# A max-pooled 3x3 convolution on one core: ten instead of eleven five-product steps, joint row sums and differences, weight taps kept as neighbours, and a new order

## The chip, the cores and the metric

The kernel runs on one core of one Trainium2 chip. The metric is the device time of one execution in microseconds. TensorE (PE), VectorE (DVE), ScalarE (ACT), GpSimd (POOL) and SyncE (SP) each work through their own list of instructions in order and wait for one another by semaphores. Transfers between the chip's memory and the core are started from the lists of SP, POOL and ACT.

## The reference

`x` has 16 images of 64 channels and 64 x 64 points, `weight` 128 x 64 taps of 3 x 3, `pool_size` is 2. What is computed:

```python
x_pad = np.pad(x, ((0, 0), (0, 0), (1, 1), (1, 1)))
for kh in range(3):
    for kw in range(3):
        conv[b, co] += weight[co, ci, kh, kw] * x_pad[b, ci, kh:kh+h, kw:kw+w]   # over b, co, ci
output[b, c, i, j] = np.max(conv[b, c, 2*i:2*i+2, 2*j:2*j+2])
```

The output is 16 x 128 x 32 x 32 in float32.

## The kernel before

**Steps.** Two images lie in the 128 partitions at once (64 channels each, the two "halves" h = 0 and 1). The 16 images make 8 pairs, each pair is cut into 4 quarters of 16 input rows, and one quarter of one pair is a step: 32 steps, each giving 8 pooled rows of both images. For a pooled row, two rows of the convolution are needed. With the three rows of taps g0, g1, g2 and the input rows x(-1), x(0), x(1), x(2), they are a = g0 x(-1) + g1 x(0) + g2 x(1) and b = g0 x(0) + g1 x(1) + g2 x(2).

`TYPES` says how each step does it.

- A **K step** (five products): `PA1` = (g2 - g1) x(1) and `PA2` = g0 x(-1) go to one accumulator; `PB1` = (g0 - g1) x(0) and `PB2` = g2 x(2) to another. Then max(a, b) is the larger of the two plus `PR` = g1 (x(0) + x(1)). The products read the bf16 copy `kx` of the input, and only the sum `ks` is computed beforehand.
- A **W step** (four products, row-transformed): `P2` works on the difference `we` = x(0) - x(1), `P0` and `P3` on the differences `wd` of rows two apart, `P1` on the sum `ws` = x(0) + x(1). These three are made from the float32 copy `wx`.

A product is three taps in the width for each half: for one half three matmuls of 64 rows of weights by up to 512 points. `product` pairs a product of half 0 with a product of half 1 (not always the same one) and issues the six matmuls alternately, so that the two halves of TensorE work side by side. Below, a **pair of products** means these six matmuls.

**Accumulators.** There are eight (`acc`, 128 x 8 x 64 float32), handed out from the list `free`. `ta` holds the first sum of a step and half, `tb` the second. `evac` (EV, ScalarE) copies the first one to SBUF as `ev` and frees it; in a W step `seed` (SE, ScalarE) has copied the first product into `tb` before. `rowmax` (MX, VectorE) takes the maximum of `tb` and `ev` into `tb`; after it the last product (`PR` or `P1`) is added to `tb`. `odd` (OD, ScalarE) copies the odd columns, and `colmax` (CM, VectorE) takes the maximum of the even columns and that copy into `o`, frees the accumulator and, with the second half, starts the store from SP's list. A product that opens an accumulator therefore waits for the EV or CM that freed it, and `PR` and `P1` wait for their MX.

**Row sums and differences.** `ks` (KS) is on VectorE, one per K step; `ws` (WS) on VectorE, as a `tensor_tensor` or, for steps in `SUM_BY_REDUCTION`, as a `tensor_reduce`; `we` (E) on VectorE for steps in `DIFF_ON_VECTOR`, else on GpSimd; `wd` (D) on GpSimd. `on_gpsimd` puts a GpSimd operation behind the last VectorE `tensor_tensor` (or cast) written before it in the order, so that the two do not start together.

**Loads.** The weights, the first 33 rows of pair 0 (`kfirst`, `ksecond`) and the rows of the first W step come first, on SP's list. The further rows of W steps (L, LB) follow there; LB is held until a cast of `kfirst` is done. K steps after the first two get their rows by converting transfers from POOL's list (LK).

**Weights.** `g0`..`GP` write seven blocks of three taps (with zero slots or ring copies `u...` between) into `wq`; T... turns two neighbouring slots at a time on TensorE, so that half 0 uses the upper and half 1 the lower half of a turned column; V... copies the result to `wt`.

**Order.** Nothing is planned at run time. The string `ORDER` is a list written out by hand, such as `P2.4.0` (product P2 of step 4, half 0) or `CM.22.0`, and each engine's list is what its entries have in that order. Eight matmuls on constants run on TensorE while the weights arrive.

Of the kernel before, what the change touches and what calls it, by code (L numbers as in the profile page):

```python
# [11 lines left out]
def kernel(  # L12
# [37 lines left out]
    d_pool = ctx.enter_context(tc.tile_pool(name="d_pool", bufs=5))  # L50
    e_pool = ctx.enter_context(tc.tile_pool(name="e_pool", bufs=5))
    ws_pool = ctx.enter_context(tc.tile_pool(name="ws_pool", bufs=5))
    ks_pool = ctx.enter_context(tc.tile_pool(name="ks_pool", bufs=4))
# [13 lines left out]
    sbuf_op = [None]  # L67

# [28 lines left out]
    def wload(s, part=None):  # L97
# [4 lines left out]
        if part == 0:  # L102
            hi = 2 * R * q + R + 1
        elif part == 1:
            lo = 2 * R * q + R + 1
        return nc.sync.dma_start(out=wx[p % NWX][:, lo + 1 : hi + 1, :], in_=rows_of(p, lo, hi))
# [8 lines left out]
    klo2, khi2 = chunk(1)  # L115
    ksecond = const.tile([128, khi2 - klo2, W], FP32)
# [16 lines left out]
    BLOCKS = {"D2": 1, "G0": 5, "D0": 9, "G2": 13, "GM": 17, "G1": 21, "GP": 25}  # L133
    D2, G0, D0, G2, GM, G1, GP = BLOCKS.values()
    RING = ("GM", "G1", "GP")
    wq = const.tile([CO, 29, CI], BF16)
    wt = const.tile([128, 28, CO], BF16)
    gsum = const.tile([CO, 3, CI], FP32)
    for s in range(0, GM, 4):
        nc.gpsimd.memset(wq[:, s, :], 0.0)  # L140
# [8 lines left out]
    def ring(m):  # L149
        s = BLOCKS[m]  # L150
        nc.gpsimd.tensor_copy(out=wq[:, s + 3, :], in_=wq[:, s, :])  # L151

    def turned_cols(m):
        lo = BLOCKS[m] - (m not in RING)
# [15 lines left out]
    def turn_out(m):  # L170
# [3 lines left out]
        if m == "GM":  # L174
            nc.scalar.mul(dst, src, 0.5)
        elif m == "GP":
            nc.vector.tensor_scalar_mul(out=dst, in0=src, scalar1=0.5)
        elif m in ("G0", "G2"):
# [4 lines left out]
    def tap_of(m0, kw, half):  # L183
        if m0 in (GM, G1, GP):
            return m0 + (kw - half) % 3
        return m0 + kw - half

    def taps(t, h, m0, rows, start=False, skip=None, span=(0, R)):
# [7 lines left out]
        def one(kw):  # L196
            o0, o1, c0, c1 = (0, W, 0, W) if kw == 1 else (1, W, 0, W - 1) if kw == 0 else (0, W - 1, 1, W)
            if start and kw == 1:
# [3 lines left out]
                wt[lo : lo + CI, tap_of(m0, kw, h), :],  # L202
# [25 lines left out]
    def q_of(s):  # L228
        return place[s][1]
# [38 lines left out]
    def first_product(k, part):  # L268
        s, q = KSTEPS[0], 0
        m0, first, where, skip = (  # L270
            (D2, 1, ta, None),
            (G0, -1, ta, 0),
# [8 lines left out]
        pair_of_taps(where, s, m0, step2(kx_of(s), first), start, skip, span)  # L281


    def second_product(k, part):
        s = WSTEPS[0]
        if k == 0 and part == 0:
            take(ta, s, 0)
            take(ta, s, 1)
        m0, of, where = ((GM, "we", ta), (G0, "wd", ta), (G2, "wd", tb))[k]
        rows = step1(row[of, s]) if k == 0 else step2(row[of, s], k - 1)  # L290
        span = (0, R // 2) if part == 0 else (R // 2, R)
        pair_of_taps(where, s, m0, rows, k == 0 and part == 0, None, span)
# [4 lines left out]
    def ks(s):  # L297
        row["ks", s] = ks_pool.tile([128, R, W], BF16, name="ks")
        t, f = kx_of(s), 2 * R * q_of(s)
        on_vector(  # L300
            nc.vector.tensor_tensor(  # L301
                out=row["ks", s], in0=t[:, f : f + 2 * R : 2, :], in1=t[:, f + 1 : f + 2 * R : 2, :], op=ADD
            )
        )
# [5 lines left out]
    def ws(s):  # L310
        row["ws", s] = ws_pool.tile([128, R, W], BF16, name="ws")
        t, f = wx_rows(s)
        if s in SUM_BY_REDUCTION:
            with nc.allow_low_precision("bf16 operand of TensorE, as the other row sums"):
                nc.vector.tensor_reduce(  # L315
                    out=row["ws", s],
                    in_=t[:, f : f + 2 * R, :].rearrange("p (r two) w -> p r w two", two=2),
# [5 lines left out]
            nc.vector.tensor_tensor(  # L323
                out=row["ws", s], in0=t[:, f : f + 2 * R : 2, :], in1=t[:, f + 1 : f + 2 * R : 2, :], op=ADD
            )
        )

    def we(s):
        row["we", s] = e_pool.tile([128, R, W], BF16, name="we")
        t, f = wx_rows(s)  # L330
        vector = s in DIFF_ON_VECTOR
        inst = (nc.vector if vector else nc.gpsimd).tensor_tensor(  # L332
            out=row["we", s], in0=t[:, f : f + 2 * R : 2, :], in1=t[:, f + 1 : f + 2 * R : 2, :], op=SUB
# [3 lines left out]
    def wd(s):  # L337
        row["wd", s] = d_pool.tile([128, 2 * R, W], BF16, name="wd")
        t, f = wx_rows(s)
        on_gpsimd(  # L340
            nc.gpsimd.tensor_tensor(  # L341
                out=row["wd", s], in0=t[:, f + 1 : f + 1 + 2 * R, :], in1=t[:, f - 1 : f - 1 + 2 * R, :], op=SUB
            )
        )

    def we_half(part):
        s = WSTEPS[0]
        if part == 0:
            row["we", s] = e_pool.tile([128, R, W], BF16, name="we")
        t, f = wx_rows(s)  # L350
        lo, hi = f + R * part, f + R * (part + 1)
        on_vector(
            nc.vector.tensor_tensor(
                out=row["we", s][:, R // 2 * part : R // 2 * (part + 1), :],
                in0=t[:, lo:hi:2, :],
                in1=t[:, lo + 1 : hi : 2, :],
                op=SUB,
            )
        )

    def wd_half(part):
        s = WSTEPS[0]
        if part == 0:
            row["wd", s] = d_pool.tile([128, 2 * R, W], BF16, name="wd")
        t, f = wx_rows(s)
        lo, hi = f + R * part, f + R * (part + 1)
        on_gpsimd(
            nc.gpsimd.tensor_tensor(
                out=row["wd", s][:, R * part : R * (part + 1), :],
                in0=t[:, lo + 1 : hi + 1, :],  # L370
                in1=t[:, lo - 1 : hi - 1, :],
                op=SUB,
            )
        )

    def lk(n, part):
# [3 lines left out]
        if n == 0:  # L380
            inst = kload(0, *chunk(2 + part))
            if part == 0:
                behind(inst, sbuf_op[0])
# [6 lines left out]
    def late_load(s):  # L390
        behind(wload(s), sbuf_op[0])
# [21 lines left out]
    def seed_half(part, h):  # L413
        s = WSTEPS[0]
        span = slice(R // 2 * part, R // 2 * (part + 1))
        if part == 0:
            t = take(tb, s, h, fresh=False)
            if t in unset:
                unset.discard(t)
                nc.tensor.matmul(  # L420
                    acc[t], zeros[:, 0:128], zeros, start=True, stop=True, skip_group_check=True
                )
        nc.scalar.copy(out=acc[tb[s, h]][:, span, :], in_=acc[ta[s, h]][:, span, :])

# [8 lines left out]
    def colmax(s, h):  # L433
        if s not in ot:
            ot[s] = o_pool.tile([128, 2, R, WO], FP32, name="o")
        t = tb.pop((s, h))
        nc.vector.tensor_tensor(out=ot[s][:, h], in0=acc[t][:, :, 0::2], in1=od[s, h], op=MAX)  # L437
        free.append(t)
        made[s] = made.get(s, 0) + 1
        p, q = place[s]  # L440
        dst = out[2 * p : 2 * p + 2, :, q * R : (q + 1) * R, :].rearrange("b c h w -> c b (h w)")
        src = ot[s].rearrange("p b h w -> p b (h w)")
        if s == N - 1:
            store = nc.scalar if made[s] == 1 else nc.sync
# [3 lines left out]


    def cast_rows(lo, hi):  # L450
        on_vector(nc.vector.tensor_copy(out=kx[0][:, lo:hi:2, :], in_=kfirst[:, lo:hi:2, :]))  # L451

    def cast_more(first):
        dst, src = kx[0][:, klo2 + first : khi2 : 2, :], ksecond[:, first::2, :]
        if first in CAST_ON_VECTOR:
# [13 lines left out]
        "XOa": lambda: cast_rows(1, kmid),  # L469
        "XOb": lambda: cast_rows(kmid, khi),  # L470
        "XEa": lambda: cast_rows(0, kmid),
        "XEb": lambda: cast_rows(kmid + 1, khi),
        "X1": lambda: cast_more(0),
        "X2": lambda: cast_more(1),
        "F": first_product,
        "G": second_product,
        "Ea": lambda: we_half(0),
        "Eb": lambda: we_half(1),
        "Da": lambda: wd_half(0),
        "Db": lambda: wd_half(1),  # L480
        "SEa": lambda h: seed_half(0, h),
# [112 lines left out]
```

## Time and profile before

| | |
|---|---|
| three runs | 104.67, 104.80, 105.44 us (median 104.8) |
| the profiled execution | 105.15 us, of which the span of the instructions is 103.4 us |
| busy in the span | PE 97.2, DVE 92.0, ACT 82.2, POOL 75.6 us |
| mean granted TensorE clock | 0.993 |
| moved by transfers | HBM read 17.14 MB, written 8.39 MB |

The page of the profile lists, for groups of instructions, the mean time of one (from its start to its end) and the busy time of all; where instructions of one engine overlap, the distance from one start to the next is shorter than the mean. That distance is what fills an engine's list, and it is read from the timeline: four MX begin at 16.03 us and the next instruction at 18.47 us, so one MX takes 0.61 us of the list though it lasts 0.69 us. In the profile, MX is line 427, CM line 437, the matmuls of products line 200, OD line 431, EV lines 399 and 401, SE line 411, WS lines 315 (reduction) and 323, E line 332, D line 341, KS line 301.

### The profile page before, as it was taken

The page shows a single profiled execution, that of the slowest core. Times are in us where ns is not written, and L with a number is a line of the kernel's source. Part 1 is how long each engine was busy: PE and PEld are TensorE (multiplying, and loading weights), DVE is VectorE, ACT ScalarE, POOL GpSimd, SP SyncE. Part 2 cuts the span into 40 slices and gives each one's busy share as a digit, 9 for nine tenths or more (in the row PEclk, how much of TensorE's full clock was granted, in tenths as well). Part 3 has the DMA queues.
Part 4 walks back from the last instruction along what each step waited for, and adds up shares of the span by engine and source line. Part 5 has one row for each costly group of instructions (what it writes and reads, how often), then busy time and mean ns, then how long its engine had stood idle before and what let it go on. Part 6 is the DMA issues. An engine that isn't in the chain of part 4 may idle for free.

```text
span 103.4 us, 2541 instructions
## 1 busy us (share of the span) xinstructions
PE 97.2 (94%) x909; PEld 62.9 (61%) x909; DVE 92.0 (89%) x179; ACT 82.2 (79%) x181; POOL 75.6 (73%) x65
## 2 busy tenths in 40 slices
PE   6999799999999999999999999999999999999910
PEld 2497655555865465576666685556746777777600
DVE  1389899999999999999999999999989996979960
ACT  4546988886789997993887898987899898698820
POOL 6046869773995899998999997959997919970000
PEclk9999999999999999999999999999999999999997
DMA  2988999999999999999859992187699232006152
GB/s 62 299 312 262 360 291 268 349 416 404 248 194 298 286 318 339 351 340 204 163 159 261 312 384 101 56 205 263 176 154 257 81 136 101 0 13 233 65 202 102
DMA packets 13341, 23.33 MB, mean 226 GB/s; under 512 B 1040, under 2 KB 9488, under 8 KB 13328
## 3 DMA queue, kind: packets, MB, share of 16 engines
q1 hardware_dynamic: 12320, 20.68, 60.8%
q0 software_dynamic: 864, 2.36, 13.7%
q8 instruction: 7, 0.11, 0.4%
q10 hardware_dynamic: 144, 0.13, 0.4%
q14 instruction: 6, 0.05, 0.1%
HBM read 17.14 MB, written 8.39 MB: 247 GB/s over the span
## 4 chain that ended last, share of the span: by engine, by line
PE 91%; DVE 3%; issue 1%; DVEq 0%
PE acc L200 85%; PE acc L551 3%; PE acc L164 2%; DVE acc L427 2%; DVE o L437 1%; DVEq L589 0%; DVEq L437 0%; DVEq L427 0%
## 5 line engine op out<-in xcount | busy, mean ns | idle before, releaser
L200 PEld LDWEIGHTS <-wt 64*128 64x128 bf16 x876 | 59.6, 94 | 31.5 <-issue 1.5
L341 POOL TENSOR_TENSOR wd<-wx 128x1024 bf16<-128x1024 f32 x20 | 47.1, 2361 | 7.7 <-PE acc L200 3.4
L200 PE MATMUL acc<-wd,wt 64*128 64x504 bf16 (+3 forms) x264 | 50.1, 367 | 0.0
L200 PE MATMUL acc<-kx,wt 64*128 64x504 bf16 (+6 forms) x288 | 50.0, 356 | 0.0
L427 DVE TENSOR_TENSOR acc<-acc,ev 128x512 f32<-128x512 f32 x64 | 42.0, 691 | 1.1 <-ACT ev L401 0.3
L200 PE MATMUL acc<-we,wt 64*128 64x512 bf16 (+2 forms) x132 | 31.7, 367 | 0.0
L200 PE MATMUL acc<-ws,wt 64*128 64x504 bf16 (+1 forms) x126 | 28.7, 377 | 0.1
L401 ACT ACTIVATE ev<-acc 128x512 f32<-128x512 f32 x42 | 25.1, 608 | 2.7 <-PE acc L200 2.3
L431 ACT COPY od<-acc 128x256 f32<-128x256 f32 x64 | 22.5, 379 | 5.8 <-PE acc L200 5.2
L437 DVE TENSOR_TENSOR o<-acc,od 128x256 f32<-128x256 f32 x64 | 24.5, 416 | 2.1 <-ACT od L431 1.9
L411 ACT COPY acc<-acc 128x512 f32<-128x512 f32 x40 | 23.0, 581 | 3.0 <-PE acc L200 1.7
L332 POOL TENSOR_TENSOR we<-wx 128x512 bf16<-128x512 f32 x16 | 20.2, 1273 | 3.3 <-DVE ws L323 2.4
L200 PE MATMUL acc<-ks,wt 64*128 64x504 bf16 (+1 forms) x66 | 16.5, 377 | 0.5 <-DVE acc L427 0.5
L315 DVE TENSOR_REDUCE ws<-wx 128x512 bf16<-128x1024 f32 x11 | 13.5, 1229 | 0.0
L399 ACT COPY ev<-acc 128x512 f32<-128x512 f32 x22 | 12.9, 595 | 0.6 <-PE acc L200 0.6
L323 DVE TENSOR_TENSOR ws<-wx 128x512 bf16<-128x512 f32 x10 | 7.1, 723 | 0.0
L301 DVE TENSOR_TENSOR ks<-kx 128x512 bf16<-128x512 bf16 x11 | 4.6, 429 | 0.3 <-ACT kx L458 0.3
L551 PE MATMUL acc<-const-bfloat16-1.0 128*128 128x512 bf16 x8 | 3.6, 628 | 0.8 <-PEq L575 0.8
L95 POOL DMA_DIRECT2D kx<-in_x_dram x6 | 3.5, 587 | 0.7 <-DVE kx L451 0.7
L164 PEld LDWEIGHTS <-wq 128*128 128x128 bf16 x25 | 2.3, 132 | 1.4 <-issue 1.4
L151 POOL COPY wq<-wq 128x64 bf16<-128x64 bf16 x3 | 0.7, 241 | 3.1 <-ACT wq L462 2.5
L164 PE MATMUL acc<-ident,wq 128*128 128x128 bf16 x25 | 2.8, 285 | 0.0
(30 smaller groups left out, 22.3 us busy)
## 6 DMA issues: line engine op xcount, KB each, us to landing
out_dram<-o SPq DMA_DIRECT2D x31, 256.0 KB, 4.2
wx<-in_x_dram SPq DMA_DIRECT2D x10, 512.0 KB, 7.2
wx<-in_x_dram SPq DMA_DIRECT2D x5, 544.0 KB, 7.6
wx<-in_x_dram SPq DMA_DIRECT2D x5, 480.0 KB, 7.4
kx<-in_x_dram POOLq DMA_DIRECT2D x2, 528.0 KB, 7.4
ksecond<-in_x_dram SPq DMA_DIRECT2D x1, 512.0 KB, 7.0
kx<-in_x_dram POOLq DMA_DIRECT2D x2, 256.0 KB, 7.0
kx<-in_x_dram POOLq DMA_DIRECT2D x1, 496.0 KB, 12.0
```

What stands on the lines that cost most here:

```text
L164: nc.tensor.transpose(tp[:, (j - lo) * CO : (j - lo + 1) * CO], wq[:, j : j + 2, :].rearrange("a b c -> a (b c)"), ident,)
L200: nc.tensor.matmul(acc[t][:, i0:i1, o0:o1], wt[lo : lo + CI, tap_of(m0, kw, h), :], rows(lo, i0, i1, c0, c1), start=start and kw == 1, sto ...
L315: nc.vector.tensor_reduce(out=row["ws", s], in_=t[:, f : f + 2 * R, :].rearrange("p (r two) w -> p r w two", two=2), axis=mybir.AxisListTy ...
L323: nc.vector.tensor_tensor(out=row["ws", s], in0=t[:, f : f + 2 * R : 2, :], in1=t[:, f + 1 : f + 2 * R : 2, :], op=ADD)
L332: inst = (nc.vector if vector else nc.gpsimd).tensor_tensor(out=row["we", s], in0=t[:, f : f + 2 * R : 2, :], in1=t[:, f + 1 : f + 2 * R : ...
L341: nc.gpsimd.tensor_tensor(out=row["wd", s], in0=t[:, f + 1 : f + 1 + 2 * R, :], in1=t[:, f - 1 : f - 1 + 2 * R, :], op=SUB)
L399: nc.scalar.copy(out=ev[s, h], in_=acc[t])
L401: nc.scalar.mul(ev[s, h], acc[t], -1.0)
L411: nc.scalar.copy(out=acc[t], in_=acc[ta[s, h]])
L427: nc.vector.tensor_tensor(out=t, in0=t, in1=ev[s, h], op=MAX)
L431: nc.scalar.copy(out=od[s, h], in_=acc[tb[s, h]][:, :, 1::2])
L437: nc.vector.tensor_tensor(out=ot[s][:, h], in0=acc[t][:, :, 0::2], in1=od[s, h], op=MAX)
```

## The change

- Types: steps 0 and 1 are now K steps and one K step fewer remains: 10 K, 22 W.
- Steps 0 and 1 have their first four products in two groups of four rows (F and H, `split_product`). The halved operations of the first W step (Ea, Eb, Da, Db, SEa, SEb, G) are gone. `ksecond` is loaded in two parts, and the first W step's rows in one.
- KS, WS, E and D can take two neighbouring steps of one pair in one instruction of twice the width (`E.4.6`, `D.8.9`, `KS.5.7`, `WS.14.15` ...); each kind gets a pool of tiles for single and one for double operations. Joint are four of the KS, six of the D, eight of the E (one of them on VectorE) and five of the WS.
- Six copies and casts change between VectorE and ScalarE (`SWAPPED`). `X2` goes to VectorE.
- `wq` has the blocks next to each other in another order, so that the last tap of one block and the first of the next are neighbours for the turning; the ring copies are gone, and 24 instead of 25 turns remain.
- `od` and `o` have 5 instead of 6 tiles. The last half's store is started by ACT, the one before by SP (before, the other way round). LB is held behind the last `kfirst` cast before it (`gate`).
- A new `ORDER`. (`colmax_once` is defined and not used in it.)

```diff
-    TYPES = "KWKWWKWKWWKWWKWKWWKWWKWWWWKWWKWW"
-    DIFF_ON_VECTOR = (3, 4, 6, 11,)
-    CAST_ON_VECTOR = ()
-    SUM_BY_REDUCTION = (1, 3, 9, 11, 12, 14, 16, 17, 19, 20, 22,)
+    TYPES = "KKWWWKWKWWKWWKWWWWKWWKWWWWKWWKWW"
+    DIFF_ON_VECTOR = (2, 3, 4, 6, 19,)
+    CAST_ON_VECTOR = (1,)
+    SWAPPED = ("VD2", "VG1", "VG2", "VGP", "XEa", "XEb",)
+    SUM_BY_REDUCTION = (2, 3, 4, 6, 9, 11, 12, 14, 15, 17, 19, 20, 22,)
...
+    bufs = {("d", 1): 4, ("d", 2): 3, ("e", 1): 3, ("e", 2): 4, ("ws", 1): 4, ("ws", 2): 3, ("ks", 1): 3, ("ks", 2): 2}
...
-    od_pool = ctx.enter_context(tc.tile_pool(name="od_pool", bufs=6))
-    o_pool = ctx.enter_context(tc.tile_pool(name="o_pool", bufs=6))
+    od_pool = ctx.enter_context(tc.tile_pool(name="od_pool", bufs=5))
+    o_pool = ctx.enter_context(tc.tile_pool(name="o_pool", bufs=5))
...
-            nc.sync.dma_start(out=ksecond, in_=rows_of(0, klo2, khi2))
+            nc.sync.dma_start(out=ksecond[:, 0:kpart, :], in_=rows_of(0, klo2, klo2 + kpart))
+            nc.sync.dma_start(out=ksecond[:, kpart:, :], in_=rows_of(0, klo2 + kpart, khi2))
         else:
-            wload(s, 0)
-            wload(s, 1)
+            wload(s)
...
-    BLOCKS = {"D2": 1, "G0": 5, "D0": 9, "G2": 13, "GM": 17, "G1": 21, "GP": 25}
+    BLOCKS = {"D0": 1, "G2": 4, "D2": 7, "G0": 10, "G1": 13, "GM": 17, "GP": 21}
...
+    def tiles_of(kind, pool, steps, rows):
+        n = len(steps)
+        t = pools[pool, n].tile([128, n * rows, W], BF16, name=f"{kind}{n}")
+        for i, s in enumerate(steps):
+            row[kind, s] = t[:, i * rows : (i + 1) * rows]
+        return t
...
-    def wd(s):
-        row["wd", s] = d_pool.tile([128, 2 * R, W], BF16, name="wd")
-        t, f = wx_rows(s)
+    def wd(*steps):
+        n = 2 * R * len(steps)
+        dst = tiles_of("wd", "d", steps, 2 * R)
+        t, f = wx_rows(steps[0])
         on_gpsimd(
-            nc.gpsimd.tensor_tensor(
-                out=row["wd", s], in0=t[:, f + 1 : f + 1 + 2 * R, :], in1=t[:, f - 1 : f - 1 + 2 * R, :], op=SUB
-            )
+            nc.gpsimd.tensor_tensor(out=dst, in0=t[:, f + 1 : f + 1 + n, :], in1=t[:, f - 1 : f - 1 + n, :], op=SUB)
         )
...
-        behind(wload(s), sbuf_op[0])
+        behind(wload(s), gate[0])
...
+        if name in SWAPPED:
+            gate[0] = nc.scalar.copy(out=dst, in_=src)
+        else:
+            gate[0] = on_vector(nc.vector.tensor_copy(out=dst, in_=src))
...
     ORDER = """
...
-        Ea KS.0 Eb EV.0.1 G.0.0 EV.0.0 G.0.1 uGP P2.3.1 SEa.0 SEa.1 SEb.1 MX.0.1 Da Db TGP SEb.0 MX.0.0 VGP
...
+        D0 D2 g2 g0 g1 XEa TD0 TG2 VD0 GS TD2 TG0 TG1 VD2 VG2 F.2.0 XOa LB.3 LB.4 LB.6 LB.8 LB.9 F.0.0 XEb
+        F.2.1 XOb VG0 F.3.0 GM GP LK.0.0 TGM TGP F.1.0 F.0.1 X2 VG1 VGM X1 F.3.1 KS.0 F.1.1 KS.1 H.0.0
+        EV.0.1 H.0.1 H.1.0 P2.2.1 EV.0.0 VGP H.1.1 E.2 D.2 H.2.0 LK.0.1 H.3.0 P2.2.0 EV.1.1 EV.1.0 MX.0.1
+        MX.0.0 WS.2 H.2.1 E.3 PR.0.0 H.3.1 PR.0.1 MX.1.1 SE.2.0 D.3 P0.2.0 P3.2.0 SE.2.1 P0.2.1 OD.0.1
...
+        LK.1.1 WS.8 PB2.5.0 P0.6.0 EV.4.0 PA1.7.1 EV.4.1 PB1.5.1 EV.6.1 KS.5.7 MX.6.1 SE.6.0 L.16 L.17
...
+        PB1.7.1 SE.8.1 MX.7.0 D.8.9 P2.8.0 E.11.12 PB2.7.1 PR.7.0 P0.8.0 OD.6.0 CM.4.0 CM.5.1 SE.8.0 P0.8.1
...
+        PB2.10.1 P0.12.0 MX.12.1 MX.14.0 E.16.17 D.15 WS.17 EV.10.1 KS.10.13 P3.12.0 PA1.13.0 SE.14.1
...
+        SE.15.1 PB2.10.0 MX.12.0 EV.13.0 PR.10.1 P1.12.0 MX.14.1 OD.10.1 OD.14.0 D.16.17 P0.15.1 P2.16.0
...
+        P0.22.1 P3.22.1 P1.20.0 P0.22.0 D.24.25 MX.21.0 EV.22.1 PR.21.1 PR.21.0 MX.22.1 OD.20.0 CM.20.0
+        OD.21.1 CM.21.1 P2.23.1 EV.22.0 P1.22.1 OD.21.0 E.27 P2.24.0 P3.22.0 P2.24.1 SE.23.1 CM.21.0 OD.22.1
...
```

More of the change, by code (lines that the diff above doesn't have):

```diff
@@ L147 @@
     turned = {}
-    def ring(m):
-        s = BLOCKS[m]
-        nc.gpsimd.tensor_copy(out=wq[:, s + 3, :], in_=wq[:, s, :])
     def turned_cols(m):
-        lo = BLOCKS[m] - (m not in RING)
+        lo = BLOCKS[m] - (m in LEADING)
         hi = BLOCKS[m] + 3
@@ L280, in first_product, with ks @@
             take(where, s, 1)
[L281 to L292, printed above, removed]
-    row = {}
-    def ks(s):
-        row["ks", s] = ks_pool.tile([128, R, W], BF16, name="ks")
-        t, f = kx_of(s), 2 * R * q_of(s)
+        rows = step2(kx_of(s), 2 * q * R + first)
+        pairs = [taps(where[s, h], h, m0, rows, start=start, skip=skip, span=span) for h in range(2)]
+        for one, other in zip(*pairs):
+            one()
+            other()
+    row = {}
+    def tiles_of(kind, pool, steps, rows):
[4 more added lines that the diff above has]
+        return t
+    def ks(*steps):
+        n = 2 * R * len(steps)
+        dst = tiles_of("ks", "ks", steps, R)
+        t, f = kx_of(steps[0]), 2 * R * q_of(steps[0])
         on_vector(
-            nc.vector.tensor_tensor(
-                out=row["ks", s], in0=t[:, f : f + 2 * R : 2, :], in1=t[:, f + 1 : f + 2 * R : 2, :], op=ADD
-            )
+            nc.vector.tensor_tensor(out=dst, in0=t[:, f : f + n : 2, :], in1=t[:, f + 1 : f + n : 2, :], op=ADD)
         )
@@ L322, in ws, with we @@
         on_vector(
-            nc.vector.tensor_tensor(
-                out=row["ws", s], in0=t[:, f : f + 2 * R : 2, :], in1=t[:, f + 1 : f + 2 * R : 2, :], op=ADD
-            )
-        )
[L328 to L331, printed above, removed]
+            nc.vector.tensor_tensor(out=dst, in0=t[:, f : f + n : 2, :], in1=t[:, f + 1 : f + n : 2, :], op=ADD)
+        )
+    def we(*steps):
+        n = 2 * R * len(steps)
+        dst = tiles_of("we", "e", steps, R)
+        t, f = wx_rows(steps[0])
+        vector = steps[0] in DIFF_ON_VECTOR
@@ L411, in seed @@
         nc.scalar.copy(out=acc[t], in_=acc[ta[s, h]])
[L413 to L423, printed above, removed]
     def rowmax(s, h):
@@ L431, in odd, with finish @@
         nc.scalar.copy(out=od[s, h], in_=acc[tb[s, h]][:, :, 1::2])
[L433 to L439, printed above, removed]
+    def finish(s, h):
         p, q = place[s]
@@ L486 @@
     for m in BLOCKS:
-        steps["u" + m] = lambda m=m: ring(m)
         steps["T" + m] = lambda m=m: turn(m)
```

246 lines of the change are left out of this document (110 added, 136 removed).

## The prediction

> **What bounds the kernel now.** I read the busy shares first, then the chain that ended last, then the timelines of TensorE and VectorE.
>
> ```profile
> PE 97.2 (94%) x909; PEld 62.9 (61%) x909; DVE 92.0 (89%) x179; ACT 82.2 (79%) x181; POOL 75.6 (73%) x65
> ...
> PE 91%; DVE 3%; issue 1%; DVEq 0%
> ```
>
> PE and VectorE are both nearly full, so the chain decides. In order of time:
>
> ```profile
> 9.68 1.31 DVE acc L427 x2
> 10.98 0.04 issue
> 11.03 64.89 PE acc L200 x609
> 75.92 0.03 issue
> 75.94 20.43 PE acc L200 x186
> 96.37 0.02 issue
> ```
>
> From 11.03 us PE runs on without a gap to 96.37, at a granted clock of 1.00. Is PE the only limit? Its rate:
>
> ```profile
> 29.80 0.38 PE L200 MATMUL acc<-wd,wt 64*128 64x512 bf16 x1
> ...
> 34.34 0.38 PE L200 MATMUL acc<-we,wt 64*128 64x512 bf16 x1
> ```
>
> Seven pairs of products lie between these two: 4.54 / 7 = 0.649 us each (0.6486 below). Now VectorE:
>
> ```profile
> 18.47 0.68 DVE L332 TENSOR_TENSOR we<-wx 128x512 bf16<-128x512 f32 x1
> 19.36 1.75 DVE L437 TENSOR_TENSOR o<-acc,od 128x256 f32<-128x256 f32 x5 [0.21 <-ACT od L431]
> 21.03 0.69 DVE L427 TENSOR_TENSOR acc<-acc,ev 128x512 f32<-128x512 f32 x1
> ...
> 41.12 1.22 DVE L315 TENSOR_REDUCE ws<-wx 128x512 bf16<-128x1024 f32 x1
> 42.26 0.82 DVE L437 TENSOR_TENSOR o<-acc,od 128x256 f32<-128x256 f32 x2
> ...
> 75.88 0.70 DVE L427 TENSOR_TENSOR acc<-acc,ev 128x512 f32<-128x512 f32 x1
> ```
>
> From start to start, a CM takes 0.334 (five from 19.36 to 21.03), a reduction 1.14, an MX 0.605 (three from 26.48 to 28.27, four from 16.03 to 18.47), a WS or E by `tensor_tensor` 0.605 (two from 22.56 to 23.77), a KS 0.335 (two from 46.55 to 47.21). Between E.4 at 18.47 and CM.22.0, which ends at 75.88, VectorE's list has 39 MX, 44 CM, 9 reductions, 5 WS, 7 KS and 3 E: 23.60 + 14.70 + 10.26 + 3.03 + 2.35 + 1.82 = 55.7 us, and it took 57.4. Only 1.7 us of 57 are waits, most of them for an `od` or `ev`, that is, for PE. And the pair that CM.22.0 frees an accumulator for (P0.24.0 with P2.25.1) begins at 75.94, where the chain has its small break. So up to 76 us PE and VectorE finish together; **a gain on PE alone is worth nothing before that point unless VectorE comes earlier too.** Behind it VectorE has room (busy 8.9 of 10 us from 80 to 90) and PE alone sets the end: 34 pairs x 0.6486 = 22.05, 75.94 + 22.05 = 98.0; the last matmul stops counting at 98.5 (it ends at 98.67, of which 0.16 is depth), so 0.5 is lost at P1.31 waiting for MX.31.
>
> **The change, part by part.**
>
> PE. One step changes from five products to four: one pair less, -0.65. Before the first product 16 instead of 19 turns of 0.112 (19 in 2.12 us): -0.3. Later 8 turns instead of 6: +0.2. The wait from 9.57 to 11.03 for MX.0.0 (1.46, with three turns of 0.34 in it) goes: the products of step 1 need only casts, and stand between step 0's and `PR.0`: -1.1. F.2.1 now waits for XEb, third in ScalarE's list: +0.1. PE alone is thus about 1.8 us better.
>
> VectorE. What is late next is this list. It starts its unbroken part with E.2, which needs the first W step's rows, now the last of the early transfers. Before, `ksecond` stood there:
>
> ```profile
> ksecond<-in_x_dram SPq DMA_DIRECT2D x1, 512.0 KB, 7.0
> ```
>
> Issued at 3.06, landed at 10.06, last of 1,888 KB; 832 KB had landed at 6.15, so 270 KB per us. Now 1,920 KB: 10.2. But LB goes out some 0.9 us earlier (XOa ends at about 6.05 instead of 6.92) and LK.0.0 some 1.0 (behind GP, not XEb), and both share the transfer engines with it. No row shows that cost: I take 0.2 (bounds 0 and 1.0): **E.2 at 10.4**. X2 and KS before it fill gaps that wait for transfers and for X1; a cast moved to ScalarE there costs nothing.
>
> From E.2 to the end of CM.20.0 the new list has 45 MX, 42 CM, 9 single and 2 joint reductions, 2 single and 1 joint WS, 3 single and 1 joint E, 3 joint KS. A joint operation is not in the trace. A CM has half the elements of an MX, so the fixed part of one is 2 x 0.334 - 0.605 = 0.06; a joint one saves that once: 2.21, 1.14, 1.14 and 0.60. The bounds, no saving or twice as much, are +-0.5 in all. Sum: 27.22 + 14.03 + 10.26 + 4.42 + 1.21 + 1.14 + 1.82 + 1.14 + 1.80 = **63.0 us**.
>
> CM.20.0 frees the accumulator of P2.24.0 (with P1.22.1); from there 38 pairs remain: 38 x 0.6486 = 24.65. PE alone would reach that pair at 6.2 + 100 pairs (64.5, first and last rows taken off) + turns and waits 1.1 = 71.8; VectorE releases it at 10.4 + 63.0 + 0.07 = 73.5. So PE waits, some 2 us in all, and the sum goes by VectorE.
>
> Waits in those 63 us: at least 0.1; at the rate of before (1.67 in 57.4) 1.9. Before, VectorE waited since it was ahead of PE; here PE is behind it, so I take 0.3, near the lower end. Tail: 0.5 as before; again two MX of step 31 stand behind P3.31.
>
> Sum: 10.4 + 63.0 + 0.07 + 0.3 + 24.65 + 0.5 = 98.9 against 98.5. The last store now goes from ACT (2.5 to landing, SP's 2.4): +0.1. **+0.5 us: span 103.9, execution 105.65** against the 105.15 of the profiled one. That one is 0.35 above the median, so 104.8 + 0.5 = **105.3**.
>
> At nothing: ScalarE's added EV, SE and casts (82.2 busy of 103 before; nearly 2 us more fit); the ring copies gone from GpSimd (0.24 each, beside PE's first products); five tiles of `od` and `o` (no wait of before names them; a store lands in 4.2 us and a tile comes round after five steps, some 13 us). Uncovered, one wait for a store would cost what is left of 4.2.
>
> **GpSimd and the joint operations.** D takes 2.36 (2361 ns), half of it 1.26, so a joint D takes 4.56; a joint E 2.36.
>
> ```profile
> 67.76 1.27 POOL L332 TENSOR_TENSOR we<-wx 128x512 bf16<-128x512 f32 x1 [0.51 <-DVE ks L301]
> 68.39 0.41 DVE L437 TENSOR_TENSOR o<-acc,od 128x256 f32<-128x256 f32 x1
> 68.72 0.87 DVE L323 TENSOR_TENSOR ws<-wx 128x512 bf16<-128x512 f32 x1
> ```
>
> A WS that starts under a GpSimd operation lasts 0.87 instead of 0.68, and ends 0.56 after that operation's end at 69.03, as if it had stood until then. The Trainium skill, page SBUF — State Buffer, section "Who interferes with whom", says that a VectorE instruction with two SBUF inputs and a GpSimd instruction that reads SBUF exclude each other and the later one fully blocks; by that rule, the trace agrees. By this row alone a meeting costs 0.2, four of them 0.8 (106.1); by the rule it costs whatever is left of the GpSimd operation, which rival 1 prices from rows.
>
> So each KS, WS or E by `tensor_tensor` can be held for what is left of GpSimd's operation, now up to 4.56. The sums between them: KS.5.7 to KS.10.13: VectorE 21.13, GpSimd (D.8.9 and seven of 2.36) 21.08; KS.10.13 to WS.16: 4.70 against 4.56; E.19 to KS.18.21: 8.25 against 8.18; KS.18.21 to WS.24.25: 6.77 against 6.92. They fit, with nothing to spare.
>
> **The rivals.**
> 1. **GpSimd late** (slower). If GpSimd waits between KS.5.7 and KS.10.13 (before, it stood 1.08 for a store and 0.41 for PE in the 21 us from 24.9 on) by more than VectorE does, D.15 is still running when KS.10.13 comes, and each us of delay is a us of VectorE, hence of the end. It decides from 0.05 us on. Price 1.5: 106.8. For it: no margin; against: fewer operations, and D starts earlier. Chance 0.24.
> 2. **The early rows land late.** Bound of 1.0 instead of 0.2: 106.1. Chance 0.13.
> 3. **PE's gain comes through** (faster), if the joint operations and swaps shorten VectorE's 63 us by 2: 71.8 + 24.65 + 0.5 + 0.1 = 97.0, -1.5: 103.3. Against: the distances repeat within 0.02 throughout the trace. Chance 0.12.
> 4. That the change doesn't shorten PE's list is excluded: its 138 pairs (139 before) can be counted.
>
> **Numbers.** The forecast, 105.3, has 0.51; its own range, by the bounds of E.2 and the waits, is 104.4 to 106.2. With the rivals, 103.9 to 107.1. About 1% (1.05 us) is what a measurement of this kernel can tell from no change: faster 0.12, within 0.52, slower 0.36 (rivals 1 and 2).
>
> **What would show it.** Right: E.2 begins near 10.4, CM.20.0 ends near 73.7, PE waits for VectorE (CM.1.1, CM.3.1, MX.8.1) between 20 and 40 us, P1.31 ends near 98.9. Wrong: PE without waits; a KS or WS lasting far above its 0.4 to 1.2 us; PE waiting for `wd` (D.11, at about 35); VectorE waiting for transfers.

## The result, and the profile after

| | before | after |
|---|---|---|
| median of 20 runs each | 104.88 us (104.39 to 105.44) | 106.16 us (105.29 to 107.51) |
| ratio | | **1.0114**, 95% interval 1.0094 to 1.0134 |
| the profiled execution | 105.15 us, span 103.4 | 106.99 us, span 105.2 |

The changed kernel is 1.1% slower, 1.3 us by the medians. The forecast was 105.3 us, +0.5. The ratios, here and below, leave out executions over 1.5% above the fastest of the same kernel: three of the 20 of the changed kernel (106.99, 106.99 and 107.51 us, one of them the profiled one) and two of the six of the kernel with four tiles below (111.04 and 111.29 us). So what this profile shows is one long execution, 0.8 us over the median, and its price for the whole kernel has to come from the experiments.

The busy shares and the chain by engine, from the page of the changed kernel:

```profile
PE 97.8 (93%) x908; PEld 57.5 (55%) x908; DVE 91.3 (87%) x165; ACT 83.5 (79%) x184; POOL 75.7 (72%) x48
...
PE 58%; DVE 16%; DMA 14%; issue 4%; POOL 2%; SPq 1%; ACT 1%; DVEq 0%
```

Before, PE held 91% of the chain and transfers none. Now VectorE holds 16% and transfers 14%. The transfer in the middle of the chain is not a load. The chain in order of time (start, length, what):

```profile
31.12 0.43 DVE o L400 x2
31.55 8.71 DMA out_dram<-o
40.27 0.02 issue
...
49.35 45.98 PE acc L193 x418
```

A store of 256 KB, started at 31.55, takes 8.71 us to land, and what follows waits for it. It is the store of step 4, whose last CM (CM.4.0, the first of the two at 31.12) has just ended; the store of step 5 starts at 32.0, when CM.5.1 is done. The timeline of VectorE says who (CM is now line 400, MX line 375, E line 325, WS lines 309 and 317, KS line 296):

```profile
10.38 0.69 DVE L325 TENSOR_TENSOR we<-wx 128x512 bf16<-128x512 f32 x1 [0.31 <-DMA wx<-in_x_dram]
...
38.76 0.41 DVE L400 TENSOR_TENSOR o<-acc,od 128x256 f32<-128x256 f32 x1
40.29 0.42 DVE L400 TENSOR_TENSOR o<-acc,od 128x256 f32<-128x256 f32 x1 [1.12 <-DMA out_dram<-o]
```

The first line is E.2, at 10.38 where 10.4 was forecast. The last is CM.8.1, the first CM of step 8. It writes a tile `o`; there are five, and steps 5, 6, 7 and 9 hold four of them, so it gets that of step 4, the first to finish. VectorE stands 1.12 us, and CM.8.1 begins right behind the landing of that store (40.27), before the store of step 5 has landed (32.0 + 8.8). The expectations below name step 5's store for this wait; the times say step 4's.

TensorE's matmuls show the price. For each stretch of 10 us: its length, then busy time and instructions of PE, PEld, DVE, ACT and POOL, the clock, the transfer engines' share and GB/s. Before:

```profile
12.00:22.00 10.00, 10.00 (x106) 5.75 (x103) 9.50 (x20) 8.70 (x20) 8.10 (x6) 1.00 1.05 324
...
32.00:42.00 10.00, 10.00 (x96) 5.70 (x94) 9.97 (x18) 9.22 (x22) 8.51 (x6) 1.00 1.00 317
```

After:

```profile
12.00:22.00 10.00, 9.60 (x89) 4.42 (x86) 10.00 (x18) 7.98 (x18) 8.63 (x5) 1.00 1.05 364
...
32.00:42.00 10.00, 9.37 (x81) 4.35 (x80) 8.88 (x17) 8.15 (x19) 10.00 (x5) 1.00 1.03 286
```

A stretch without waits has 96 matmuls (of the six stretches of before from 32 to 92 us five have 96 and one 93). After the change PE misses some 7 in the first stretch, where VectorE's list holds it, as forecast, and 15 in the stretch with the store; the same kernel with six tiles `o` (below) misses 4 and 6 there, so about 9 of the 15 go with the store. PE's busy time hides most of this, since a matmul that stands behind a wait still counts up to its modelled end; **the count of instructions shows a starved engine sooner than its busy share.**

### The profile page after: what moved, and what is told of

It reads as the page before. It is cut to its first block, busy times and chain, and to the rows that moved or that the text cites. A ratio compares the mean times of both kernels' runs of the same rounds, so it can differ in the third digit from the quotient of the medians.

```text
span 105.2 us, 2502 instructions
## 1 busy us (share of the span) xinstructions
PE 97.8 (93%) x908; PEld 57.5 (55%) x908; DVE 91.3 (87%) x165; ACT 83.5 (79%) x184; POOL 75.7 (72%) x48
## 4 chain that ended last, share of the span: by engine, by line
PE 58%; DVE 16%; DMA 14%; issue 4%; POOL 2%; SPq 1%; ACT 1%; DVEq 0%
PE acc L193 58%; DMA out_dram<-o 8%; DVE acc L375 7%; DMA ksecond<-in_x_dram 6%; DVE o L400 3%; DVE ws L309 3%; POOL wd L335 2%; DVE ws L317 1%; DVE ks L296 1%; DVE we L325 1%; ACT kx L430 1%; SPq L112 0%; SPq L111 0%; SPq L107 0%; DVEq L554 0%
## 5 line engine op out<-in xcount | busy, mean ns | idle before, releaser
L193 PEld LDWEIGHTS <-wt 64*128 64x128 bf16 x876 | 55.1, 94 | 38.6 <-issue 5.5
L335 POOL TENSOR_TENSOR wd<-wx 128x1024 bf16<-128x1024 f32 (+1 forms) x16 | 50.6, 3170 | 9.7 <-DVE we L325 4.5
L193 PE MATMUL acc<-wd,wt 64*128 64x504 bf16 (+1 forms) x264 | 51.5, 377 | 0.7 <-POOL wd L335 0.3
L193 PE MATMUL acc<-kx,wt 64*128 64x504 bf16 (+6 forms) x288 | 42.4, 338 | 0.3 <-ACT kx L430 0.2
L193 PE MATMUL acc<-we,wt 64*128 64x512 bf16 (+1 forms) x132 | 32.9, 377 | 0.1
L193 PE MATMUL acc<-ws,wt 64*128 64x512 bf16 (+1 forms) x132 | 31.7, 377 | 0.4 <-DVE acc L375 0.4
L325 POOL TENSOR_TENSOR we<-wx 128x1024 bf16<-128x1024 f32 (+1 forms) x10 | 20.4, 2039 | 4.1 <-DVE ks L296 2.8
L309 DVE TENSOR_REDUCE ws<-wx 128x512 bf16<-128x1024 f32 (+1 forms) x11 | 15.6, 1428 | 0.0
L317 DVE TENSOR_TENSOR ws<-wx 128x512 bf16<-128x512 f32 (+1 forms) x6 | 5.9, 987 | 0.0
L296 DVE TENSOR_TENSOR ks<-kx 128x1024 bf16<-128x1024 bf16 (+1 forms) x6 | 3.5, 595 | 0.0
```

Of the source, the lines that this page charges most:

```text
L193: nc.tensor.matmul(acc[t][:, i0:i1, o0:o1], wt[lo : lo + CI, m0 + kw - h, :], rows(lo, i0, i1, c0, c1), start=start and kw == 1, stop=True ...
L296: nc.vector.tensor_tensor(out=dst, in0=t[:, f : f + n : 2, :], in1=t[:, f + 1 : f + n : 2, :], op=ADD)
L309: nc.vector.tensor_reduce(out=dst, in_=t[:, f : f + n, :].rearrange("p (r two) w -> p r w two", two=2), axis=mybir.AxisListType.X, op=ADD,)
L317: nc.vector.tensor_tensor(out=dst, in0=t[:, f : f + n : 2, :], in1=t[:, f + 1 : f + n : 2, :], op=ADD)
L325: inst = (nc.vector if vector else nc.gpsimd).tensor_tensor(out=dst, in0=t[:, f : f + n : 2, :], in1=t[:, f + 1 : f + n : 2, :], op=SUB)
L335: nc.gpsimd.tensor_tensor(out=dst, in0=t[:, f + 1 : f + 1 + n, :], in1=t[:, f - 1 : f - 1 + n, :], op=SUB)
```

## The experiments

Three theories. **Stores:** the five tiles of `o`, left at nothing in the forecast, hold VectorE. **GpSimd:** its joint operations of 4.5 us hold VectorE or bring operands late (rival 1). **VectorE's list:** what is left of the loss is the length of its list, as summed in the forecast.

### Tiles of o and od

Six tiles of `o` with the new order:

```diff
-    o_pool = ctx.enter_context(tc.tile_pool(name="o_pool", bufs=5))
+    o_pool = ctx.enter_context(tc.tile_pool(name="o_pool", bufs=6))
```

> The changed kernel with six output tiles instead of five, nothing else. Store theory (VectorE's CM.8.1 stands 1.1 to 1.2 us for the store of step 5, whose tile it needs, and that moves everything behind it): about 0.8 to 1.1 us less than the changed kernel, so 105.1 to 105.4, some 0.3 to 0.5 us above the kernel before; no idle time of VectorE before a CM on a store; CM.20.0 ends near 73.9 in the trace. GpSimd theory (the joint operations hold VectorE): no change, 106.2.

Measured: 105.28 us, ratio 1.0059 (1.0029 to 1.0090), against 104.66 for the kernel before on that chip.

Six tiles of `od` with five of `o`:

```diff
-    od_pool = ctx.enter_context(tc.tile_pool(name="od_pool", bufs=5))
+    od_pool = ctx.enter_context(tc.tile_pool(name="od_pool", bufs=6))
```

> The changed kernel with six tiles for the odd columns instead of five, the output tiles left at five. Store theory: no change, 106.2, the wait at CM.8.1 stays. If the smaller number of buffers as such were the cause, whichever they are: about 0.8 us less.

Measured: 105.77 us, 1.0105 (1.0068 to 1.0142): as slow as the change itself.

Four tiles of `o`:

```diff
-    o_pool = ctx.enter_context(tc.tile_pool(name="o_pool", bufs=5))
+    o_pool = ctx.enter_context(tc.tile_pool(name="o_pool", bufs=4))
```

> The changed kernel with four output tiles: a second dose. Store theory: a tile comes round one step sooner, some 3 us, so that several CM wait for stores in the stretch with full transfer engines (up to about 45 us), and not only there: 2 to 5 us more than with five, 108 to 111. GpSimd theory: no change.

Measured: 1.0384 (1.0324 to 1.0445); the four executions that this counts have a median of 108.76 us. Its waits, by VectorE line and releaser (us in total, times, longest):

```profile
DVE o L400 <- DMA out_dram<-o: 3.4, 2, 2.5
```

One is again ahead of CM.8.1 (0.83, for the store of step 5 this time), the longer one ahead of CM.16.1 (2.53, for that of step 10).

Five tiles of `o` in the kernel before, with the old order:

```diff
-    o_pool = ctx.enter_context(tc.tile_pool(name="o_pool", bufs=6))
+    o_pool = ctx.enter_context(tc.tile_pool(name="o_pool", bufs=5))
```

> The kernel before with five output tiles instead of six. From its trace, a tile would come round 5.7 us after its store's issue at the soonest (step 23 after 20, at 80 us, where stores land in 4 us) and 8.5 to 9.1 us in the stretch with full engines (steps 11 and 8). Store theory: 0 to 0.4 us more than before, since the first CM of a step comes later behind the store five steps back than in the new order. If five tiles as such cost what the change lost: 1 us more.

Measured: 104.84 us, 1.0012 (0.9983 to 1.0041): nothing.

What follows. The sixth tile is worth 0.49 us by the medians of the kernels with six `o` and with six `od` (105.77 - 105.28). The intervals of these two just overlap, but the result (1.0114) lies clear of the six-tile kernel (1.0059). The fifth tile is worth some 3.0 us (108.76 - 105.77), and the sixth tile of `od` nothing that can be seen. It is having five tiles **together with the new order** that costs: in the old order it is free. Where the sixth tile is there, VectorE runs through the same place without standing:

```profile
38.82 0.74 DVE L400 TENSOR_TENSOR o<-acc,od 128x256 f32<-128x256 f32 x2
39.56 0.70 DVE L375 TENSOR_TENSOR acc<-acc,ev 128x512 f32<-128x512 f32 x1
```

Here CM.9.1 and CM.8.1 follow each other with no wait. The kernel with six tiles of `od` and five of `o` shows the same in its profiled execution (CM.9.1 and CM.8.1 from 38.85 on, without a wait), because in that execution step 4's store, started at 31.62, landed in 6.2 us instead of 8.7; its span is 104.2 against 105.2. So the wait is not in every execution. It depends on how long the store takes: step 4's took 8.7 us in the changed kernel, 7.6 with six `o` and 6.2 with six `od`, one execution each, and VectorE comes for the tile 7.6 us after the start of the store (39.17 - 31.55). The next reuse is nearly as tight: CM.11.0 takes step 5's tile some 8.1 us after the start of its store, and that store took 8.8, 8.5 and 7.6 us in the same three. How often a wait comes in the other executions isn't shown: of the two traces with five tiles and the new order one has it.

### Joint operations

Six tiles of `o`, and the joint operations taken apart:

```diff
-    P1.2.0 E.4.6 ... WS.4.6 ... KS.5.7 ... D.8.9 ... E.11.12 ... WS.24.25 ...
+    P1.2.0 E.4 E.6 ... WS.4 WS.6 ... KS.5 KS.7 ... D.8 D.9 ... E.11 E.12 ... WS.24 WS.25 ...
```

> Six output tiles, and every joint sum or difference of two steps is made as two single operations again, in the same places of the order (more small buffers for them). Theory A (the joint operations were priced rightly: each saves about 0.065 us of VectorE, seven of them before the end of CM.20.0, and VectorE's list still decides up to there): 0.3 to 0.6 us slower than the six-tile kernel, about 1.010 of the kernel before. Rival B (GpSimd's joint operations of 4.5 us hold VectorE or bring operands late): 0.3 us or more faster than the six-tile kernel, at or below 1.003. Rival C (TensorE waits for the differences of step 11 at 35 us and nothing else counts): +0.1 us, 1.007, since the single operations end there only 0.13 later.

Measured: 107.10 us, 1.0235 (1.0207 to 1.0263), 1.8% above the six-tile kernel, each against the kernel before on its own chip. Rivals B and C fall: joint operations help, with the sign of theory A and three times its size. By the timelines, VectorE was 0.41 us later at the CM ahead of WS.24 (69.24 instead of 68.83). That is what theory A priced, but partly by luck, since this execution had begun E.2 1.04 us earlier than the other (9.35 against 10.39). Then WS.24 and WS.25 took from 69.92 to 71.44 instead of 69.50 to 70.65, 0.37 more, because the first came under a GpSimd difference that ran to 70.37. That makes 0.8, and the span is 0.9 longer than with six tiles (105.0 against 104.1). The other 0.9 of the medians isn't in these two traces: the profiled execution here is the shortest of its four (106.77), that of the six-tile kernel the longest of its twelve (105.91).

### GpSimd

Six tiles, and the row difference of step 19 moved to GpSimd, joint with that of step 20:

```diff
-    DIFF_ON_VECTOR = (2, 3, 4, 6, 19,)
+    DIFF_ON_VECTOR = (2, 3, 4, 6,)
...
-        ... P0.16.0 SE.16.1 E.19 CM.14.1 ... PR.13.0 P1.15.1 E.20 P1.16.0
+        ... P0.16.0 SE.16.1 CM.14.1 ... PR.13.0 P1.15.1 E.19.20 P1.16.0
...
-        ... L.27 E.22.23 L.28 LK.2.0 EV.15.0 ... MX.17.1 SE.17.0 ... CM.15.0 KS.18.21
+        ... L.27 EV.15.0 ... MX.17.1 KS.18.21 E.22.23 L.28 LK.2.0 SE.17.0 ... CM.15.0
```

> Six output tiles; the row difference of step 19 moves from VectorE to GpSimd, in one joint operation with that of step 20, and the joint column-pair sum of steps 18 and 21 stands ahead of GpSimd's next joint difference. That takes 0.605 us off VectorE's list at 53 us. Theory A (VectorE's list decides up to 74 us): 0.3 to 0.6 us faster than the six-tile kernel, 1.000 to 1.003 of the kernel before. Rival C (TensorE, after its wait at 35 us, alone sets the end): within 0.15 us of the six-tile kernel, 1.005 to 1.007. Rival B (GpSimd is at its limit): slower by 0.3 or more, since 1.1 us are added to GpSimd.

Measured: 107.17 us, 1.0244 (1.0217 to 1.0272): 0.605 us off VectorE's list, and 1.9 us slower by the medians. Theory A's number fails and rival B's comes, but the traces show that the edit did two things at once. GpSimd with six tiles:

```profile
55.06 4.53 POOL L335 TENSOR_TENSOR wd<-wx 128x2048 bf16<-128x2048 f32 x1
59.54 2.39 POOL L325 TENSOR_TENSOR we<-wx 128x1024 bf16<-128x1024 f32 x1
...
62.75 4.57 POOL L335 TENSOR_TENSOR wd<-wx 128x2048 bf16<-128x2048 f32 x1 [0.30 <-PE acc L193]
```

and with the difference moved, with VectorE's KS.18.21 as the last line:

```profile
55.58 4.54 POOL L335 TENSOR_TENSOR wd<-wx 128x2048 bf16<-128x2048 f32 x1
61.13 2.36 POOL L325 TENSOR_TENSOR we<-wx 128x1024 bf16<-128x1024 f32 x1 [1.01 <-PE acc L193]
...
64.04 4.53 POOL L335 TENSOR_TENSOR wd<-wx 128x2048 bf16<-128x2048 f32 x1
...
60.23 0.69 DVE L296 TENSOR_TENSOR ks<-kx 128x1024 bf16<-128x1024 bf16 x1
```

The joint differences of steps 22 and 23 (D.22.23) end 1.25 us later, at 68.57. The added work explains only a part: D.19.20 ends 0.53 later (60.12 against 59.59). Then GpSimd stands 1.01 us ahead of E.22.23, where it did not stand before. The profile puts that idle time down to TensorE, but this edit also moved E.22.23 behind KS.18.21, and `on_gpsimd` holds it until that sum ends, at 60.92. A shorter pause ahead of D.22.23 takes 0.3 back. TensorE, then VectorE, in the same kernel:

```profile
68.62 0.37 PE L193 MATMUL acc<-wd,wt 64*128 64x512 bf16 x1 [0.73 <-POOL wd L335]
```

```profile
69.89 0.42 DVE L400 TENSOR_TENSOR o<-acc,od 128x256 f32<-128x256 f32 x1 [0.78 <-ACT od L379]
70.23 1.74 DVE L317 TENSOR_TENSOR ws<-wx 128x1024 bf16<-128x1024 f32 x1
```

P0.23.0 waits 0.73 us for `wd`; VectorE then waits 0.78 for an `od` that comes later, and its joint sum WS.24.25 lasts 1.74 instead of 1.22 because GpSimd's next difference runs until 70.88. 0.73 + 0.52 = 1.25, and the span is 1.3 longer (105.4 against 104.1). With six tiles the same `wd` ended at 67.32 and was needed at 67.77. So GpSimd has 0.45 us of slack there, and a `wd` that comes later than that does cost, as rival 1 of the forecast says. That GpSimd's work is at its limit isn't shown: by an estimate from the same rows this `wd` would have ended at about 67.6 without the idle time (68.57 - 1.01), in time. Nor did the work taken off VectorE help before that point. At CM.10.1 this execution is 0.14 us ahead of the six-tile one (50.40 against 50.54), and at WS.20, behind the missing E.19, it is 0.15 ahead (56.90 against 57.05): in between VectorE waited for TensorE's sums. The hold of 0.52 is nearly all that was left of GpSimd's operation (0.65 from 70.23). By the rule of the Trainium skill, page SBUF — State Buffer, section "Who interferes with whom", the later of the two is blocked for the whole rest; the trace agrees within 0.13 us.

Six tiles, and the neighbour differences of step 11 earlier:

```diff
-        PB1.7.1 SE.8.1 MX.7.0 D.8.9 P2.8.0 E.11.12 PB2.7.1 ... WS.11 P0.11.0 D.11 EV.9.1
+        PB1.7.1 SE.8.1 MX.7.0 D.8.9 P2.8.0 E.11 D.11 E.12 PB2.7.1 ... WS.11 P0.11.0 EV.9.1
```

> Six output tiles; the joint row difference of steps 11 and 12 on GpSimd is split, and the neighbour differences of step 11 stand between its halves, so that they end 1.1 us earlier (about 34.2 instead of 35.3 us). VectorE's list is unchanged. Theory A (VectorE's list decides): within 0.2 us of the six-tile kernel, 1.004 to 1.008 of the kernel before; its wait at 35 us gone, TensorE waits for VectorE instead. Rival C (the wait for GpSimd at 35 us is what is left of the loss): 0.3 us or more faster than the six-tile kernel, below 1.003.

Measured: 105.51 us, 1.0071 (1.0041 to 1.0102): no gain, as theory A said. In the six-tile kernel PE does wait for this `wd`, and from there the chain runs through PE alone:

```profile
32.98 2.35 POOL wd L335
35.33 0.04 issue
35.37 58.88 PE acc L193 x538
```

With the earlier `wd` the wait for GpSimd at 35 us is gone from the chain, and the median is not better. A wait that the chain passes through can be worth nothing when another limit lies just behind it.

Both of these together:

> Both: six output tiles, step 19's row difference on GpSimd, and the neighbour differences of step 11 ahead of the row difference of step 12. Theory A: as with the first of the two alone, 1.000 to 1.003 of the kernel before. If the two limits (VectorE's list, and TensorE's wait for GpSimd at 35 us) lie within 0.3 us of each other, only this one gains: 0.6 us faster than the six-tile kernel, 1.000, where each alone gains under 0.3. Rival B: slower than the six-tile kernel by 0.3.

Measured: 106.78 us, 1.0208 (1.0181 to 1.0236). The edit with the moved difference decides alone.

### VectorE's list

Six tiles, and two maxima made twice at 54 and 58 us:

```diff
-        ... EV.16.0 MX.13.0 MX.16.0 ...   ... P2.20.1 MX.15.0 PA2.21.1 ...
+        ... EV.16.0 MX.13.0 MX.13.0 MX.16.0 ...   ... P2.20.1 MX.15.0 MX.15.0 PA2.21.1 ...
```

> Six output tiles; two of VectorE's maxima (MX.13.0 and MX.15.0, at 54 and 58 us) are made twice, which changes no value and adds 2 x 0.605 = 1.21 us to VectorE's list ahead of CM.20.0. Theory A (VectorE's list sets the end up to CM.20.0): 0.9 to 1.3 us slower than the six-tile kernel, 1.014 to 1.018 of the kernel before. Rival C (TensorE alone sets the end from 35 us on): at most 0.5 us slower, up to 1.010.

Measured: 106.62 us, 1.0173 (1.0130 to 1.0217). Against the six-tile kernel's 1.0059 that is 1.14%, 1.2 us: theory A. In the trace a second MX begins 0.73 us after the first, whose result it needs, so that the two add about 1.45 us to the list and not 1.21. Of these 1.44 arrive at CM.20.0: it begins 1.12 later than with six tiles (74.49 against 73.37), in an execution that began E.2 0.32 earlier. PE's matmuls from 52 to 62 us fall from 95 to 83. That TensorE alone sets the end (at most 1.010) is out. But VectorE alone doesn't set it either: from 42 to 72 us the six-tile kernel's TensorE runs at its full rate (97, 95 and 96 matmuls in 10 us each), and the moved difference above gained nothing there. Up to CM.20.0 both lists are full; work added to VectorE costs, while work taken off it alone was not seen to help. The matmuls that the six-tile kernel misses are missed before 42 us (92, 94 and 90 from 12 to 42).

The same behind CM.20.0:

```diff
-        ... PA2.26.0 MX.25.1 SE.27.1 ... E.28 MX.25.0 CM.23.0 ...
+        ... PA2.26.0 MX.25.1 MX.25.1 SE.27.1 ... E.28 MX.25.0 MX.25.0 CM.23.0 ...
```

> Six output tiles; MX.25.1 and MX.25.0 (at 81 to 84 us, behind CM.20.0) are made twice, again 1.21 us of VectorE. Theory A: VectorE has room there (9.0 of 10 us busy from 72 to 82, and it waits for TensorE's sums), so 0 to 0.4 us slower than the six-tile kernel, 1.006 to 1.010 of the kernel before. If VectorE sets the end all the way, it costs the same as the two early ones, 1.014 or more.

Measured: 106.71 us, 1.0172 (1.0127 to 1.0218). A miss: by the times, the late work costs as much as the early. VectorE with six tiles:

```profile
80.78 0.70 DVE L375 TENSOR_TENSOR acc<-acc,ev 128x512 f32<-128x512 f32 x1
81.59 0.42 DVE L400 TENSOR_TENSOR o<-acc,od 128x256 f32<-128x256 f32 x1
82.09 0.70 DVE L375 TENSOR_TENSOR acc<-acc,ev 128x512 f32<-128x512 f32 x1
82.70 0.41 DVE L400 TENSOR_TENSOR o<-acc,od 128x256 f32<-128x256 f32 x1
83.03 1.47 DVE L317 TENSOR_TENSOR ws<-wx 128x1024 bf16<-128x1024 f32 x1
```

and with the late maxima (this execution runs 0.31 us ahead of the other one from the start):

```profile
80.47 1.43 DVE L375 TENSOR_TENSOR acc<-acc,ev 128x512 f32<-128x512 f32 x2
81.81 0.41 DVE L400 TENSOR_TENSOR o<-acc,od 128x256 f32<-128x256 f32 x1
82.14 1.42 DVE L375 TENSOR_TENSOR acc<-acc,ev 128x512 f32<-128x512 f32 x2
83.47 0.41 DVE L400 TENSOR_TENSOR o<-acc,od 128x256 f32<-128x256 f32 x1
83.80 1.22 DVE L317 TENSOR_TENSOR ws<-wx 128x1024 bf16<-128x1024 f32 x1
```

From the first MX to the joint sum it is 2.25 us without and 3.33 with the two extra MX, which again add 1.45 to the list (the chain has the second ones at 81.20 and 82.86): 1.08 come through. The other 0.37 are the two gaps of the first listing, 0.2 ahead of a CM that waits for its `od` and 0.17 ahead of an MX that waits for its `ev`; the extra work fills them. PE's matmuls from 82 to 92 us fall from 95 to 85, and the chain of this kernel goes through all four MX to PE at 83.61. So "VectorE has room there" was read wrongly from its busy share: there was room for a quarter of the work, and beyond it TensorE waits.

Six tiles, and the loads for steps 4, 6, 8 and 9 some 3 us later:

```diff
-        ... F.2.0 XOa LB.3 LB.4 LB.6 LB.8 LB.9 F.0.0 XEb ...  VGM X1 F.3.1 ...
+        ... F.2.0 XOa LB.3 F.0.0 XEb ...  VGM X1 LB.4 LB.6 LB.8 LB.9 F.3.1 ...
...
-            on_vector(nc.vector.tensor_copy(out=dst, in_=src))
+            gate[0] = on_vector(nc.vector.tensor_copy(out=dst, in_=src))
```

> Six output tiles; of the five loads that stand behind the second cast, four (for steps 4, 6, 8 and 9) wait for the cast of the second slab instead, some 3 us later, so that the rows of step 2 share the transfer engines with one load and not with five. Theory A: E.2, which waits for those rows at 10.39, begins at 9.9 to 10.1 (the sums KS.0 and KS.1 end at 10.0), VectorE's whole list comes 0.3 to 0.4 earlier, 0.3 us faster than the six-tile kernel, 1.002 to 1.004 of the kernel before. Against it: the four loads land 3 us later, and if VectorE then waits for the rows of step 4 or 6 (E.4.6 at about 18 to 20 us) it is slower than the six-tile kernel.

Measured: 105.45 us, 1.0056 (1.0021 to 1.0092). The gain of 0.3 isn't seen, though the interval doesn't exclude it. E.2 begins at 10.00 here, but at 10.07 and 10.09 in the two kernels with doubled maxima, on the same chip and with early loads. The rows of step 2 landed 6.91 us after their issue, against 6.98 and 6.99. That would make the other loads cost E.2 less than 0.1 us, but single executions can't tell: with early loads E.2 begins anywhere from 9.35 to 10.39 in the traces of these runs, and with late loads at 9.49 in the next one.

Eight tiles of `o`, the late loads and the earlier `wd` of step 11 in one:

> Eight output tiles, the four loads late, and the neighbour differences of step 11 ahead of the row difference of step 12. Theory A (what is left of the loss is VectorE's list alone, and six output tiles already free it of stores): the same as the kernel with the late loads, within 0.2 us. If stores still hold VectorE with six tiles in some executions, it is 0.3 us or more faster than that one, at or below the kernel before (1.000).

Measured: 105.30 us, 1.0049 (1.0017 to 1.0080): as theory A said, the same as with late loads alone. No gain from more than six tiles is seen, nor from an E.2 that begins 0.51 us earlier (9.49): CM.8.1 begins at 38.74 in both. No version of the changed kernel here beats the kernel before.

## Why the prediction was wrong

The forecast, 105.3, was +0.5 us, with a chance of 0.52 for a change of less than about 1%; the result is +1.1%. That 106.16 us lies inside the forecast's own range (104.4 to 106.2) is luck: its width came from E.2 and from waits for TensorE, not from stores. **The step that failed is the term at nothing: "five tiles of `od` and `o` (no wait of before names them; a store lands in 4.2 us and a tile comes round after five steps, some 13 us)".** Both halves of its reason were wrong for the place that counts.

- 4.2 us is the usual landing. The view of the tile `o` in the kernel **before** would have shown the spread:

```profile
DMA to landing us min/median/max: 2.1/4.0/8.1
```

  Two stores take 8.1, started at 14.40 and 26.59 us, when the transfer engines are full (share 1.05 from 12 to 32 us). The cost of a wait stands with the slowest transfer of that stretch, not with the median.
- 13 us is the average time for five steps. But the tile is taken by the first CM of a step and let go by the landing of the store that its last CM starts, and steps 4, 5, 6 and 7 end close together: in the new order only 7.6 us lie between step 4's store and CM.8.1. In the old order, counted the same way, five tiles leave at least 9.1 us between 22 and 40 us (step 8 after step 3); in the trace of that kernel with five tiles the store there took 8.3, so it went free by 0.8 us.
- The last sentence, "uncovered, one wait for a store would cost what is left of 4.2", had the mechanism: it costs what is left of 8.7 after 7.6, 1.1 us, in the one execution where it was caught, and 0.5 to 0.6 in the median (105.77 - 105.28; 1.0114 against 1.0059).

With six tiles the kernel takes 105.28, +0.62 us against its own runs of before, where +0.5 was forecast. The rest of the sum therefore holds within the interval (0.3 to 0.9 us):

- **E.2 at 10.4:** 10.38, but 9.35 to 10.39 over the traces with these loads, so that the agreement within 0.02 is luck. No run shows the 0.2 for loads that share the transfer engines: the late loads moved E.2 by less than it varies.
- **Joint operations 2.21, 1.14, 1.14, 0.60:** from start to start WS.4.6 takes 2.24 after the change, E.4.6 1.13, WS.24.25 1.15 with six tiles, KS.5.7 0.60:

```profile
18.78 1.21 DVE L325 TENSOR_TENSOR we<-wx 128x1024 bf16<-128x1024 f32 x1
19.91 0.75 DVE L400 TENSOR_TENSOR o<-acc,od 128x256 f32<-128x256 f32 x2
...
22.17 2.31 DVE L309 TENSOR_REDUCE ws<-wx 128x1024 bf16<-128x2048 f32 x1
24.41 0.40 DVE L400 TENSOR_TENSOR o<-acc,od 128x256 f32<-128x256 f32 x1
...
25.34 0.67 DVE L296 TENSOR_TENSOR ks<-kx 128x1024 bf16<-128x1024 bf16 x1
25.94 2.48 DVE L375 TENSOR_TENSOR acc<-acc,ev 128x512 f32<-128x512 f32 x4
```

- **CM.20.0 ends at 73.7:** 73.8 with six tiles (it begins at 73.37 and lasts 0.41); 74.85 after the change, 1.1 later, the store's wait.
- **PE waits for VectorE between 20 and 40 us:** matmuls are missing as shown, in short waits and from 12 us on. What the doubled maxima cost (1.44 of 1.45 by CM.20.0) shows that VectorE's list has no room up to there, as the sum assumed.
- **38 pairs x 0.6486 behind it:** the last matmuls end at 99.10 with six tiles, less the 0.16 of depth 98.9, as forecast. But the reason given, that PE alone sets the end there, is wrong: of 1.45 us put on VectorE only 0.37 found room. It didn't matter here, since PE keeps its rate there with six tiles (95 matmuls from 82 to 92 us).
- **Rival 1, GpSimd late:** not what happened. Up to CM.20.0 no joint KS or WS lasts longer than it should (0.67 and 1.22 with six tiles), and GpSimd waits for VectorE 1.06 to 2.17 us ahead of D.16.17. With six tiles D.22.23 had 0.45 us to spare; the edit that moved E.19 shows what it costs to use up more than that.
- **The wait for D.11 at about 35**, named as a sign of being wrong, came (0.34 us with six tiles), and taking it away gained nothing that the times show.

What stays open: in how many executions VectorE waits for a store; why executions of the six-tile kernel differ by 0.9 us, though its one trace has no such wait, and with it half of what the single operations cost; whether the moved difference would have gained with E.22.23 left in its place; and which transfer made that store take 8.7 instead of 6.2 us.

## What to carry to other kernels

A buffer pool is priced where a reuse leaves least over the landing of its store, not at the averages (here 7.6 us against 8.7, and not 13 against 4.2; a reuse after 6.9, by step 16, was harmless since that store took 2.8): take, in the new order, the time from the start of each store to the first write that reuses its tile, and set it against the slowest landing of that stretch. When two engines hand accumulators to each other, idle time of either is not all room: put known work into it, or follow what the wait waits for. An edit that moves work from one engine to another often also moves what waits for what: before the result is put down to the work, look in the trace for idle time that the new order brought.

## What was unexpected of the hardware

The same 256 KB store, at the same place of the order, landed in 6.2, 7.6 and 8.7 us in executions of three kernels that differ in their numbers of tiles alone, and the fastest store in 2.1. In the stretch of that store the transfer engines were full (share 1.03) at 286 GB/s, while from 12 to 22 us the same share (1.05) moved 364.
